# Second layer's input projection: 512-column groups, per-row-block weight tiles, three token tiles side by side

## The chip, the cores and the metric

The kernel runs on one core of one Trainium2 chip. The metric is the device time of one execution in microseconds (us), taken as the median of several runs. Engines go by the profile's short names: PE (TensorE matmul) and PEld (its weight loads), DVE (VectorE), ACT (ScalarE), POOL (GpSimd) and SP (SyncE, which here only issues DMAs).

## What is computed

One inference step of a two-layer encoder on a prompt of 2048 tokens and a sample of 32 tokens, width 1024. Only the second layer's projections, its gates and the 32-token attention are rewritten by the change:

```python
def fox_layer(x, k_prefix, v_prefix, logf_prefix, norm_g, w_in, b_forget, qn_g, kn_g, w_out):
    n, t, _ = x.shape
    h = rms_norm(x, norm_g)
    proj = h @ w_in
    q, k, v, gate, fpre = jnp.split(proj, [MIX_C, 2 * MIX_C, 3 * MIX_C, 4 * MIX_C], axis=-1)
    q = rms_norm(q.reshape(n, t, FOX_HEADS, HEAD_DIM), qn_g)
    k = rms_norm(k.reshape(n, t, FOX_HEADS, HEAD_DIM), kn_g)
    v = v.reshape(n, t, FOX_HEADS, HEAD_DIM)
    logf = jax.nn.log_sigmoid(fpre.astype(F32) + b_forget.astype(F32))
    ...
    return x + (attn * jax.nn.silu(gate)) @ w_out, k, v, logf
```

The matrix `w_in` has 4 x 1024 + 16 columns: queries, keys, values, gates and one forget gate for each of 16 heads. The attention that follows weighs keys by a running sum of the forget gates.

## The kernel before

Every float32 product is made of three matmuls: both operands are split into an upper part `hi` and a rest `lo` (`split`, L153: a cast, then a subtraction), and hi x hi, hi x lo and lo x hi are summed in PSUM (the accumulator memory). The width of 1024 is cut into `KT` = 8 row blocks of 128, so that one 128-token tile of one column group takes 24 matmuls.

The second layer's projection is an object of class `Proj` (L174). `load` (L219) reads the transposed, normalized activations `h1T` in 17 transfers (sixteen of 128 tokens and one of 32) through three staging buffers `hst`, and splits each into the resident tiles `h0` to `h5` (ACT casts, DVE subtracts); the 2080 tokens lie in six `PIECES` (256, four times 384, 288). `weights` (L231) reads one column group, row block by row block, through three staging buffers `wst`, multiplies each by the norm's weight (L242), and splits it into one large tile `whl` that holds the whole group. There are two such tiles: while one is multiplied, the next is filled, by POOL alone save for the first group (DVE and ACT).

There are sixteen groups of 256 columns: four of values (V; the last has 16 forget-gate columns more), four of queries (Q), four of keys (K), four of gates (G). For V, Q and K, `token_major` (L259) takes two token tiles at a time, into the two halves of one PSUM bank of 512 columns (`pm`, four banks), 48 matmuls of 256 columns; the sample's 16 matmuls come last. V's results are copied out (L774, ACT), split and stored. Q's and K's go through `head_norm` (L306: square on ACT L309, reduce L311, small steps, a product L314 on DVE, a product L315 on POOL) and one step later through `turn` (L321), four transposes per bank, a split into `qhl` and stores to `qT` or `kT`. Between V and Q stands the log-forget section: its small tiles have a pool of their own, its two matmul pairs and three transposes (L829, L830, L841) share PSUM with others.

For the gates, `col_chunk` (L289) makes the transposed product: 128 gate columns by one piece of tokens, 24 matmuls, 48 units in all. Between units runs `sample_pair` (L900), the 32-token attention for a pair of heads, as a generator in six steps, eight pairs, one begun every four units. Each engine carries out its instructions in the order of its list, which a scheduler made; SP's list holds nearly all DMAs.

The three buffers of a pair that matter below, as they are before:

```python
            pr = wk.tile([2 * NS, 5 * P], F32, name="prs", tag="prs")
            ...
            ph = wk.tile([P, 5, 2 * NS], F32R, name="phs", tag="phs")
            ...
            op = wk.tile([2 * NS, P], F32, name="ops", tag="ops")
```

## Time and profile before

| what | value |
|---|---|
| runs | 2676.01, 2676.89, 2681.09 us (median 2676.89) |
| profiled execution, first to last instruction (span) | 2675.6 us |
| PE busy in the span | 2586.7 us, 97% |
| PEld, DVE, ACT, POOL busy | 88%, 60%, 44%, 43% |
| second layer's V, Q, K projections | about 821 to 1424 us in the span |
| its gates | about 1424 to 1639 us |
| last: attention and output projection | 1639 to 2676 us |

The profiled execution's span is 1.3 us below the median of the three runs; what lies around the span is not more than that. Busy shares are averages over stages with different limits, so a stage is read by its own stretch of the trace.

### The profile page before, as it was taken

The page shows a single profiled execution, that of the slowest core. Times are in us where ns is not written, and L with a number is a line of the kernel's source. Part 1 is how long each engine was busy: PE and PEld are TensorE (multiplying, and loading weights), DVE is VectorE, ACT ScalarE, POOL GpSimd, SP SyncE. Part 2 cuts the span into 40 slices and gives each one's busy share as a digit, 9 for nine tenths or more (in the row PEclk, how much of TensorE's full clock was granted, in tenths as well). Part 3 has the DMA queues.
Part 4 walks back from the last instruction along what each step waited for, and adds up shares of the span by engine and source line. Part 5 has one row for each costly group of instructions (what it writes and reads, how often), then busy time and mean ns, then how long its engine had stood idle before and what let it go on. Part 6 is the DMA issues. An engine that isn't in the chain of part 4 may idle for free. (4 is left out here: it accounts for less than half of the span.)

```text
span 2675.6 us, 47345 instructions
## 1 busy us (share of the span) xinstructions
PE 2586.7 (97%) x17259; PEld 2345.5 (88%) x17259; DVE 1604.6 (60%) x3847; ACT 1166.4 (44%) x2424; POOL 1149.9 (43%) x1583
## 2 busy tenths in 40 slices
PE   6999999799998999999999999999999999999999
PEld 6999999688887999999999998887888878877787
DVE  7650244778765115554553324889988988888521
ACT  5321111556554122222222114777777777777310
POOL 4454240455534434554554422555555555553100
PEclk9999999799998999999999999999999999999999
DMA  6342110976738443445555316544354455443642
GB/s 187 101 110 88 44 47 23 211 185 169 181 100 266 161 159 97 105 111 132 144 146 139 94 62 162 145 113 122 97 148 120 102 120 141 111 103 90 194 149 75
DMA packets 314120, 338.14 MB, mean 126 GB/s; under 512 B 32311, under 2 KB 263887, under 8 KB 313886
## 3 DMA queue, kind: packets, MB, share of 16 engines
q1 hardware_dynamic: 233550, 242.82, 31.6%
q0 software_dynamic: 76320, 87.98, 15.1%
q10 hardware_dynamic: 4016, 4.31, 0.5%
q8 instruction: 136, 2.23, 0.4%
q14 instruction: 98, 0.80, 0.1%
HBM read 203.05 MB, written 132.06 MB: 125 GB/s over the span
## 5 line engine op out<-in xcount | busy, mean ns | idle before, releaser
L271 PE MATMUL pm<-whl,h 128*128 128x256 f32 (+1 forms) x5760 | 713.7, 283 | 6.3 <-ACT h L155 3.1
L271 PEld LDWEIGHTS pm<-whl,h 128*128 128x128 f32 x5760 | 694.9, 190 | 7.9 <-ACT h L155 3.5
L296 PE MATMUL pm<-h,whl 128*128 128x384 f32 (+2 forms) x2880 | 472.3, 322 | 0.0
L296 PEld LDWEIGHTS pm<-h,whl 128*128 128x128 f32 x2880 | 455.3, 188 | 1.8
L158 POOL TENSOR_TENSOR pl<-pf,ph 128x512 fp32r<-128x512 f32 (+3 forms) x270 | 303.6, 1127 | 263.5 <-DVE ph L157 253.2
L1058 ACT ACTIVATE pr<-pr,mnf 128x128 f32<-128x128 f32 (+15 forms) x256 | 309.6, 1211 | 61.6 <-DVE mnf L1053 60.6
L1077 PE MATMUL pt<-ident,pr 128*128 128x128 f32 x2176 | 323.3, 274 | 5.5 <-DVE pl L158 5.4
L1077 PEld LDWEIGHTS pt<-ident,pr 128*128 128x128 f32 x2176 | 251.2, 141 | 39.3 <-DVE pl L158 11.4
L158 DVE TENSOR_TENSOR pl<-pt,ph 128x512 fp32r<-128x512 f32 (+3 forms) x436 | 261.4, 612 | 39.8 <-ACT ph L155 36.7
L1048 PE MATMUL ps<-ka,qs 128*128 128x512 f32 (+3 forms) x640 | 253.6, 397 | 16.9 <-DVE mnf L1053 15.9
L1053 DVE CUSTOM_DVE_ANT_0 pr<-ps,cb 128x1024 f32<-128x1024 f32 (+7 forms) x256 | 248.8, 981 | 17.9 <-PE ps L1049 9.2
L155 ACT CAST ph<-pt 128x512 fp32r<-128x512 f32 (+3 forms) x436 | 224.9, 529 | 60.9 <-PE pt L1077 44.0
L1070 PE MATMUL pa<-pl,vhl 128*128 128x512 f32 (+3 forms) x640 | 249.2, 395 | 2.3 <-POOL pl L158 2.3
L1070 PE MATMUL pa<-ph,vhl 128*128 128x512 f32 (+3 forms) x640 | 243.6, 383 | 3.8 <-DVE ph L157 3.2
L1049 PE MATMUL ps<-kb,qs 128*128 128x512 f32 (+3 forms) x640 | 228.8, 366 | 0.0
L1082 ACT COPY pf<-pt 128x512 f32<-128x512 f32 (+3 forms) x270 | 140.3, 523 | 66.9 <-PE pt L1077 63.9
L157 DVE CAST ph<-pf 128x512 fp32r<-128x512 f32 (+3 forms) x270 | 143.9, 537 | 35.8 <-ACT pf L1082 35.7
L577 PE MATMUL po<-wo,mh 128*128 128x512 f32 x512 | 162.9, 398 | 0.8 <-ACT mh L155 0.5
L1048 PEld LDWEIGHTS ps<-ka,qs 128*128 128x128 f32 x640 | 121.2, 189 | 46.5 <-DVE mnf L1053 30.3
L157 POOL CAST whl<-wst 128x256 fp32r<-128x256 f32 (+1 forms) x184 | 73.3, 420 | 186.3 <-PE pm L281 105.5
L242 POOL TENSOR_SCALAR wst<-wst,g1c 128x256 f32<-128x256 f32 (+1 forms) x120 | 115.5, 968 | 88.2 <-DMA wst<-in_w_in_dram 86.4
L311 DVE TENSOR_REDUCE ssh<-sq 128x8 f32<-128x512 f32 (+3 forms) x99 | 62.4, 630 | 137.3 <-ACT sq L309 137.2
(396 smaller groups left out, 4050.9 us busy)
## 6 DMA issues: line engine op xcount, KB each, us to landing
qT<-qhl SPq DMA_DIRECT2D x192, 128.0 KB, 2.4
qs<-qT POOLq DMA_DIRECT2D x48, 512.0 KB, 7.3
wst<-in_w_in_dram SPq DMA_DIRECT2D x168, 128.0 KB, 2.6
kT<-qhl SPq DMA_DIRECT2D x128, 128.0 KB, 2.4
ka<-kT POOLq DMA_DIRECT2D x32, 512.0 KB, 7.1
kb<-kT POOLq DMA_DIRECT2D x64, 256.0 KB, 9.0
cb<-cT SPq DMA_DIRECT2D x32, 512.0 KB, 9.6
vhl<-vH POOLq DMA_DIRECT2D x32, 512.0 KB, 4.7
```

Source lines behind the costliest of these rows:

```text
L155: nc.scalar.copy(hi, src)
L157: eng_hi.tensor_copy(hi, src)
L158: eng_lo.tensor_tensor(out=lo, in0=src, in1=f32(hi), op=ALU.subtract)
L271: nc.tensor.matmul(ps[:, j, :], a[:, kt, :], b[:, kt, :], start=(i == 0), stop=(i == 3 * KT - 1))
L296: nc.tensor.matmul(ps, a[:, kt, c:c + P], b[:, kt, :], start=(i == 0), stop=(i == 3 * KT - 1))
L577: nc.tensor.matmul(ps, a[:, kt, :], wo[kt][:, b, cs], start=(i == 0), stop=(i == 3 * KT - 1))
L1048: nc.tensor.matmul(ps[:, s0:s0 + m], lhs, ka[:, ks], start=True, stop=False)
L1049: nc.tensor.matmul(ps[:, s0:s0 + m], lhs, kb[:, ks], start=False, stop=not diag)
L1053: nc.vector.tensor_tensor_reduce(out=pr[:, c0:c0 + n], in0=ps[:, :n], in1=cb[:, :n], scale=1.0, scalar=mns[-1][:, 0:1] if mns else 3e38, o ...
L1058: nc.scalar.activation(pr[:, :L], pr[:, :L], AF.Exp, bias=mns[-1][:, 0:1], scale=-1.0, accum_out=sm)
L1070: nc.tensor.matmul(pa[:, r0 * P:], vhl[b], pp[:, r0:].rearrange("p r q -> p (r q)"), start=(b == 0 and i == 0), stop=(b == nkb - 1 and i = ...
L1077: nc.tensor.transpose(pt[:, r, :], prs[r][:, b * P:(b + 1) * P], ident)
```

## The change

The second layer uses a new class `WideProj`; the first layer, the attention and the output projections stay as they are.

- Groups: V in 384, 384 and 256 + 16 columns; Q, K and G in two groups of 512 each: nine groups in place of sixteen.
- Weights: ten tiles `whl`, each for one row block of one group (8 in use, 2 spare). The first two row blocks of the next group are made early, in the spare tiles; block k + 2 is written when the matmuls of the group's last token tile (or last gate unit) have used block k. Even blocks are made by POOL, odd ones by DVE, ACT and DVE; the very first group goes through DVE and ACT. Staging has two buffers `wst`, not three.
- Order of matmuls: the first three token tiles (or gate units) of a group are accumulated at the same time in three banks, row block by row block; the others one after the other. The sample comes before the last token tile.
- Each bank now holds one token tile of up to 512 columns, and `turn_wide` turns one token tile: four transposes, and stores with runs of 128 tokens (512 bytes) instead of 256 tokens.
- `load` writes straight into the `lo` tile and splits in place, with no staging buffers. It stands behind the first group's weights, as before.
- Memory: the log-forget section takes its tiles out of the two `qhl` buffers; in `sample_pair`, `prs`, `phs`, `pls` and `ops` share buffers with `ckp`, `khi`, `klo` and `qps`; the gates' `sg` has two buffers, not three.

```diff
         def load(self, srcT):
...
+            for c0, n in [(c0, P) for c0 in range(0, NTOK, P)] + [(NTOK, NS)]:
+                hi = self.at(0, c0, n)
+                lo = self.at(1, c0, n)
+                nc.sync.dma_start(f32(lo), srcT[:, c0:c0 + n].rearrange("(k p) t -> p k t", p=P))
+                split(hi, lo, f32(lo), nc.scalar, nc.vector)
...
+    class WideProj(Proj):
+        SPARE = 2
+        LEAD = 3
+
+        def slot(self, k, fast):
+            cols = self.plan[0]
+            width = sum(n for _, n in cols)
+            hl = self.wp.tile([P, 2, self.cw], F32R, name="whl", tag="whl", bufs=KT + self.SPARE)[:, :, :width]
+            st = self.wp.tile([P, self.cw], F32, name="wst", tag="wst", bufs=2)[:, :width]
...
+                nc.sync.dma_start(st[:, at:at + n], self.w[k * P:(k + 1) * P, c0:c0 + n])
...
+            (nc.vector if fast else nc.gpsimd).tensor_scalar_mul(st, st, self.g[:, k:k + 1])
+            split(hl[:, 0], hl[:, 1], st, *((nc.scalar, nc.vector) if fast else (nc.gpsimd, nc.gpsimd)))
...
+        def prefetch(self, plan, fast=False):
...
+            for k in range(KT):
+                self.slot(k, True)
+
+        def next_weights(self):
+            self.w8, self.ahead = self.ahead, []
+            for k in range(self.SPARE if self.plan else 0):
+                self.slot(k, False)
...
+        def freed(self, k):
+            if self.plan and k + self.SPARE < KT:
+                self.slot(k + self.SPARE, k % 2 == 1)
...
+            lead = [psum() for _ in range(self.LEAD)]
+            for kt in range(KT):
+                for t in range(self.LEAD):
+                    self.token_mms(lead[t], t, kt)
+            for t in range(self.LEAD):
+                out(lead[t], t)
...
+            ps = psum()
+            for kt in range(KT):
+                self.token_mms(ps, NT - 1, kt)
+                self.freed(kt)
...
-        pj = Proj(es, w_in1, g1c, "c", CW + 16, "right")
+        pj = WideProj(es, w_in1, g1c, "c", 512, "right")
...
+        vcols = [[(2048, 384)], [(2432, 384)], [(2816, 256), (4096, 16)]]
+        pj.prefetch(vcols + [[(b + c * 512, 512)] for b in (0, 1024, 3072) for c in range(2)])
         pj.load(h1T)
...
+                self.t = [pj.ev.tile([P, 1024], F32, name="lf", tag="qhl", bufs=2) for _ in range(2)]
...
-            pr = wk.tile([2 * NS, 5 * P], F32, name="prs", tag="prs")
+            pr = wk.tile([2 * NS, 5 * P], F32, name="prs", tag="ckp")
...
-            ph = wk.tile([P, 5, 2 * NS], F32R, name="phs", tag="phs")
-            pl = wk.tile([P, 5, 2 * NS], F32R, name="pls", tag="pls")
+            ph = wk.tile([P, 5, 2 * NS], F32R, name="phs", tag="khi")
+            pl = wk.tile([P, 5, 2 * NS], F32R, name="pls", tag="klo")
...
-            op = wk.tile([2 * NS, P], F32, name="ops", tag="ops")
+            op = wk.tile([2 * NS, P], F32, name="ops", tag="qps")
```

Three places where the instruction lists show the change. The first is SP's list where the second layer begins, before the change. `hst` is a load of 128 tokens of activations, `wst` one of a weight block, `h1T` the store of the last activations.

```order
L239 DMA wst_9401<-in_w_in1_dram 128x256
L239 DMA wst_9406<-in_w_in1_dram 128x256
L239 DMA wst_9411<-in_w_in1_dram 128x256
L223 DMA hst_9444<-h1T_66 128x8x128
L728 DMA h1T_66<-hT_9279 128x8x128
L223 DMA hst_9448<-h1T_66 128x8x128
L223 DMA hst_9452<-h1T_66 128x8x128
L239 DMA wst_9416<-in_w_in1_dram 128x256
```

And the same place of SP's list after the change, where the activations go straight to `h0`, `h1` and so on.

```order
L348 DMA wst_9401<-in_w_in1_dram 128x384
L348 DMA wst_9407<-in_w_in1_dram 128x384
L838 DMA h1T_66<-hT_9279 128x8x128
L348 DMA wst_9413<-in_w_in1_dram 128x384
L348 DMA wst_9419<-in_w_in1_dram 128x384
L348 DMA wst_9425<-in_w_in1_dram 128x384
L348 DMA wst_9431<-in_w_in1_dram 128x384
L348 DMA wst_9437<-in_w_in1_dram 128x384
L348 DMA wst_9443<-in_w_in1_dram 128x384
L225 DMA h0_9373<-h1T_66 128x8x128 x2
L225 DMA h1_9374<-h1T_66 128x8x128 x3
```

The first three activation loads stood behind three weight blocks; now all of them stand behind all eight, which pass through two staging buffers.

The second place is PE's list in the first Q group, before: `pm` is a bank of two token tiles, `pss` and the `pt` of L841 belong to the log-forget section.

```order
L271 MATMUL pm_11920<-whl_11056,h1_9374 128x256 x24
L271 MATMUL pm_11920<-whl_11056,h2_9375 128x256 x17
L841 MATMUL pt_11709<-ident_87,off_11691 128x128
L829 MATMUL pss_11725<-lsh_11721,upper_11651 128x80
L830 MATMUL pss_11725<-lsh_11721,ones_11654 128x80
L271 MATMUL pm_11920<-whl_11056,h2_9375 128x256 x7
L271 MATMUL pm_11997<-whl_11056,h2_9375 128x256 x12
L841 MATMUL pt_11714<-ident_87,off_11691 128x128
```

And after: banks 11359 to 11361 are token tiles 0 to 2, side by side, 11502 is tile 3 and 11555 is tile 4.

```order
L376 MATMUL pm_11359<-whl_11247,h0_9373 128x512 x3
L376 MATMUL pm_11360<-whl_11247,h0_9373 128x512 x3
L376 MATMUL pm_11361<-whl_11247,h1_9374 128x512 x3
L376 MATMUL pm_11502<-whl_11238,h1_9374 128x512 x2
L376 MATMUL pm_11502<-whl_11247,h1_9374 128x512 x3
L971 MATMUL pt_11322<-ident_87,lf_11273 128x128
L959 MATMUL pss_11334<-lf_11273,lf_11272 128x80
L960 MATMUL pss_11334<-lf_11273,lf_11272 128x80
L971 MATMUL pt_11326<-ident_87,lf_11273 128x128
L376 MATMUL pm_11555<-whl_10673,h1_9374 128x512 x3
```

The log-forget transposes stood among a bank's 48 matmuls; now they stand together, with tile 3 already used up ahead of them, and tile 4 (which takes the bank of tile 0) behind them.

The third place is PE's list at a sample pair's beginning among the gates, before: `ckp` and `qps` are the pair's keys and queries as loaded, `ops` is the pair before's result.

```order
L296 MATMUL pm_18915<-h2_9375,whl_17965 128x384 x8
L917 MATMUL pss_18948<-ident_87,ckp_18902 128x128 x4
L918 MATMUL pss_18948<-ident_87,ckp_18902 128x32
L919 MATMUL pss_18948<-ident_87,qps_18905 128x32
L296 MATMUL pm_18969<-h3_9376,whl_17965 128x384 x8
L964 MATMUL pt_18944<-ident_87,ops_18900 128x64
```

And after, at the switch to the second gate group: banks 16363 to 16365 are its three units side by side, 16525 the fourth, `whl_16326` is row block 6 and `whl_16335` row block 7.

```order
L1047 MATMUL pss_16010<-ident_87,ckp_15964 128x128 x4
L1048 MATMUL pss_16010<-ident_87,ckp_15964 128x32
L426 MATMUL pm_16363<-h0_9373,whl_16326 128x256 x2
L426 MATMUL pm_16364<-h0_9373,whl_16326 128x256 x2
L426 MATMUL pm_16365<-h0_9373,whl_16326 128x256 x2
L426 MATMUL pm_16525<-h0_9373,whl_16326 128x256 x2
L1094 MATMUL pt_16006<-ident_87,ops_15962 128x64
L1049 MATMUL pss_16010<-ident_87,qps_15967 128x32
L426 MATMUL pm_16363<-h0_9373,whl_16326 128x256
```

The transpose of the loaded `qps` stood ahead of the transpose of the old `ops`; now it stands directly behind it, and the two tiles share one buffer.

## Rows read from the trace of the kernel before

**Rows 1.** The page's first part: busy time, share of the span, instructions.

```profile
PE 2586.7 (97%) x17259; PEld 2345.5 (88%) x17259; DVE 1604.6 (60%) x3847; ACT 1166.4 (44%) x2424; POOL 1149.9 (43%) x1583
```

**Rows 2.** Windows: busy time of each engine, then granted clock, DMA share, GB/s.

```profile
850.00:1050.00 200.00, 200.00 (x1662) 199.90 (x1662) 54.38 (x149) 47.26 (x101) 76.74 (x108) 1.00 0.48 155
1050.00:1425.00 375.00, 375.00 (x3182) 375.00 (x3181) 199.70 (x529) 90.18 (x201) 190.93 (x236) 1.00 0.54 128
```

**Rows 3.** Timeline of ACT, copies of V banks: start, duration, what, idle before.

```profile
876.02 0.59 ACT L774 COPY vt<-pm 128x512 f32<-128x512 f32 x1 [5.34 <-PE pm L271]
...
915.96 0.59 ACT L774 COPY vt<-pm 128x512 f32<-128x512 f32 x1 [4.62 <-PE pm L271]
923.55 0.59 ACT L774 COPY vt<-pm 128x512 f32<-128x512 f32 x1 [5.34 <-PE pm L271]
```

**Rows 4.** Timeline of ACT, head norms' squares of Q and K banks.

```profile
1250.78 0.60 ACT L309 ACTIVATE sq<-pm 128x512 f32<-128x512 f32 x1 [1.84 <-PE pm L271]
...
1269.18 0.60 ACT L309 ACTIVATE sq<-pm 128x512 f32<-128x512 f32 x1 [3.52 <-PE pm L271]
```

**Rows 5.** Timeline of ACT, gate units of 384 columns.

```profile
1603.94 0.49 ACT L982 ACTIVATE sg<-pm 128x384 f32<-128x384 f32 x1 [3.82 <-PE pm L296]
...
1633.25 0.49 ACT L982 ACTIVATE sg<-pm 128x384 f32<-128x384 f32 x1 [3.69 <-PE pm L296]
```

**Rows 6.** Timeline of DVE, second output projection, 24 matmuls of 512 columns each.

```profile
2557.52 0.69 DVE L1205 TENSOR_TENSOR op<-ps,op 128x512 f32<-128x512 f32 x1 [3.13 <-PE ps L1196]
...
2595.60 0.69 DVE L1205 TENSOR_TENSOR op<-ps,op 128x512 f32<-128x512 f32 x1 [4.75 <-PE ps L1196]
```

**Rows 7.** Timeline of SP's issues where the second layer begins.

```profile
796.52 2.21 SPq L239 DMA_DIRECT2D wst<-in_w_in_dram  x3
802.16 0.38 SPq L223 DMA_DIRECT2D hst<-h1T  x1
...
808.61 9.13 SPq L239 DMA_DIRECT2D wst<-in_w_in_dram  x6
```

**Rows 8.** Timeline of PE in the same stretch.

```profile
817.46 0.80 PE L271 MATMUL pm<-whl,h 128*128 128x256 f32 x2 [3.09 <-ACT h L155]
820.93 11.33 PE L271 MATMUL pm<-whl,h 128*128 128x256 f32 x78 [2.67 <-DVE h L158]
```

**Rows 9.** Timeline of DVE in the same stretch.

```profile
807.97 0.41 DVE L158 TENSOR_TENSOR whl<-wst,whl 128x256 fp32r<-128x256 f32 x1
...
811.53 0.75 DVE L720 TENSOR_SCALAR hn<-xr,br 128x1024 f32<-128x1024 f32 x1 [2.00 <-POOL br L150]
...
825.84 1.23 DVE L158 TENSOR_TENSOR h<-hst,h 128x1024 fp32r<-128x1024 f32 x1 [1.08 <-ACT h L155]
```

**Rows 10.** Windows of that stretch, columns as in Rows 2.

```profile
822.00:824.00 2.00, 2.00 (x11) 2.00 (x11) 2.00 (x4) 0.00 (x0) 1.85 (x3) 0.50 0.89 244
824.00:826.00 2.00, 2.00 (x15) 2.00 (x14) 0.92 (x2) 1.05 (x1) 0.48 (x1) 0.73 1.08 303
```

**Rows 11.** Groups of POOL by form, 1050 to 1425: busy, mean ns, idle before.

```profile
L242 POOL TENSOR_SCALAR wst<-wst,g1c 128x256 f32<-128x256 f32 x56 | 51.2, 924 | 14.3 <-DMA wst<-in_w_in_dram 14.0
L158 POOL TENSOR_TENSOR whl<-wst,whl 128x256 fp32r<-128x256 f32 x56 | 40.2, 740 | 0.0
...
L157 POOL CAST whl<-wst 128x256 fp32r<-128x256 f32 x58 | 21.6, 402 | 24.1 <-PE pm L281 24.1
```

**Rows 12.** Groups of POOL by form, 1640 to 2600.

```profile
L158 POOL TENSOR_TENSOR pl<-pf,ph 128x512 fp32r<-128x512 f32 x195 | 252.3, 1294 | 186.5 <-DVE ph L157 176.4 <-PE pt L1077 9.5
```

**Rows 13.** DMA issues, 800 to 1640: count, size, median us from issue to landing.

```profile
wst<-in_w_in_dram SPq DMA_DIRECT2D x125, 128.0 KB, 2.7
...
hst<-h1T SPq DMA_DIRECT2D x16, 512.0 KB, 5.6
...
ckp<-in_cache_fox_k_dram SPq DMA_DIRECT2D x8, 256.0 KB, 3.1
...
qps<-q SPq DMA_DIRECT2D x8, 16.0 KB, 2.3
```

**Rows 14.** Groups of DVE by form, 1050 to 1425.

```profile
L314 DVE TENSOR_TENSOR hno<-pm,rr 128x512 f32<-128x512 f32 x59 | 40.7, 689 | 8.4 <-DVE rr L134 3.7 <-PE pt L326 0.4 <-DMA wst<-in_w_in_dram 0.4
L311 DVE TENSOR_REDUCE ssh<-sq 128x8 f32<-128x512 f32 x59 | 40.5, 686 | 103.7 <-ACT sq L309 103.6
L133 DVE SCALAR_TENSOR_TENSOR rt<-rt,rv 128x8 f32<-128x8 f32 x59 | 13.2, 225 | 2.0
```

More of the change, by code (lines that the diff above doesn't have):

```diff
@@ L332, in turn, with turn_wide @@
+    def turn_wide(pt, ev, o, t, h0, dstT):
+        pt = pt.rearrange("p (h t) -> p h t", h=4)
+        for hp in range(4):
+            nc.tensor.transpose(pt[:, hp], o[:, hp * P:(hp + 1) * P], ident)
+        hl = ev.tile([P, 2, 4, P], F32R, name="qhl", tag="qhl", bufs=2)
+        split(hl[:, 0], hl[:, 1], pt, nc.scalar, nc.vector)
+        for hh in range(2):
+            for w in range(2):
+                store(dstT[h0 + hh:h0 + 8:2, w, :, t * P:(t + 1) * P].rearrange("h d t -> d h t"),
                       f32(hl[hh * HD:(hh + 1) * HD, w]))
@@ L971, in hybrid_step_kernel @@
         unit = 0
-        for gc in range(4):
+        for gc in range(2):
             if gc:
-                whi, wlo = pj.next_weights()
+                pj.next_weights()
+                first = pj.col_chunks([(cc * P, 0) for cc in range(pj.LEAD)])
             for tch in range(NTC):
-                for cc in range(2):
-                    r0 = gc * CW + cc * P
-                    ps = first if unit == 0 else pj.col_chunk(whi, wlo, cc * P, tch)
+                for cc in range(4):
+                    r0 = gc * 512 + cc * P
+                    ps = first.pop(0) if first else pj.col_chunks([(cc * P, tch)], tch == NTC - 1 and cc == 3)[0]
                     c0, n = PIECES[tch]
-                    sg = pe.tile([P, TCH], F32, name="sg", tag="sg", bufs=3)[:, :n]
+                    sg = pe.tile([P, TCH], F32, name="sg", tag="sg", bufs=2)[:, :n]
                     nc.scalar.activation(sg, ps, AF.Tanh, scale=0.5)
```

149 lines of the change are left out of this document (104 added, 45 removed).

## The prediction

> **What bounds the kernel now.** I read the page's busy shares first: PE 97%, everything else far below [rows 1]. An average can hide a stage with another limit, so next come the windows of the stage that is changed: PE is busy for all of 850 to 1050 and all of 1050 to 1425, at full clock, with DVE at 27% and 53% and POOL at 38% and 51% [rows 2]. So in V, Q and K nothing but PE's own list sets the end. Faster matmuls there are worth their full difference, and every wait that PE does not have today is a loss of its full length. The working therefore has two halves: what PE's list gets shorter by, and where PE will have to wait.
>
> **The saving.** The pace of the old matmuls is read where PE sets the beat of another engine. Seven gaps between V copies last 39.94 us, 5.706 us for the 48 matmuls of a bank of 256 columns, 118.9 ns each; the gap with the sample's 16 matmuls in it is 7.59, so these take 1.88 [rows 3]. In Q and K three gaps last 18.40, 6.133 each, which is 48 matmuls and four transposes of together 0.43 [rows 4]. For 384 columns there are the gate units: seven gaps in 29.31, 4.187 for 24 matmuls, 174.5 ns [rows 5]. For 512 columns the nearest is the second output projection, whose operands alternate in the same hi, hi, lo pattern: seven gaps in 38.08, 5.44 for 24, 226.7 ns [rows 6]. Two matmuls of 256 thus cost 237.8 and one of 512 226.7: 11 ns are saved for each that goes.
> - V: three groups of 256 took 3 x 8 x 5.706 = 136.9; two of 384 take 2 x 16 x 4.187 = 134.0. The group of 272 is as it was. Saved 2.9.
> - Q and K: 8 groups x 8 x 5.706 = 365.2; 4 groups x 16 x 5.44 = 348.2. Saved 17.0. The transposes are 256 before and after.
> - Sample: 12 x 1.88 = 22.6; by the same paces 16 x (2 x 0.1745 + 0.125 + 4 x 0.2267) = 22.1. Saved 0.5.
> - Gates: the same 1152 matmuls of the same pieces. Nothing.
>
> Sum: 20.4 us, 0.76%. Bounds of the 512 pace: if each fell only as the step from 256 to 384 says (55.6 ns for 128 columns, so 230.1 for 512) the saving would be 15.2; more than 20.4 no row gives.
>
> A rule stands against this. "TensorE: Matmul & The Clock Gate", section Back-to-back issue gap, of the Trainium skill puts the gap of an isolated matmul at columns / 2.4 + 2.5 ns. By it only 2.5 ns would go with each of 1920 matmuls fewer, 4.8 us in all. The trace does not agree at 256 columns: it has 118.9 ns where the rule has 109.2.
>
> **Where PE will wait.** (1) The start. Before, three weight blocks were issued at 796.5, an activation load from 802.16, and the remaining blocks took SP until 817.7 [rows 7]; PE ran without a gap from 820.93 [rows 8]. After, SP's list puts all eight blocks ahead of the first activation load, through two buffers: blocks 2 and 3 wait for the subtractions of 0 and 1 (before, these ended at 808.4 [rows 9]), land about 2.7 later [rows 13], and are scaled behind DVE's 811.53 instruction; with cast and subtraction blocks 4 and 5 are issued at about 813.4, blocks 6 and 7 one such round later at 818.1, the first activations at 818.7. These land 4 to 5 us later (5.6 is the median with three in flight [rows 13]), are cast and then subtracted (1.23 [rows 9], and not much less for the cast): PE runs from about 825.5, 4.6 late. Between 3 (it lands early) and 8 (it waits its turn behind 0.4 MB of weights). Behind that wait on SP stand the other loads and V's first stores: 0.5, from 0 to 3.
>
> (2) Weights at a switch. T is the end of the old group's last matmul. PE needs block k of the new group 9k matmuls later, 2.04 us per block at 512 columns. POOL makes blocks 2, 4, 6: scaling and cast of 512 are taken as twice those of 256, 1.85 and 0.80 [rows 11], the subtraction is 1.29 [rows 12], 3.9 together; the load of 256 KB takes 3.1, as `ckp` of that size [rows 13]. Block 2 is loaded and scaled ahead; its place is free at T - 4.8 (the last tile's 24 matmuls take 5.44), so it is ready at T - 2.7 and gives up its staging buffer. Block 4 follows 7.0 later at T + 4.3 (needed at 8.2), block 6 at T + 11.3 (needed at 12.2). It just holds: 0.5 each for Q's second group and K's two. In V the same sum with 384 and 272 columns leaves block 6 late by 0.35 and 0.55: 0.9. For the first gate group a unit's share is 9 x 0.119 = 1.07 per block, so block 6 would be wanted at 6.4; five late turns (2.1) and the fourth unit's first 18 matmuls (2.1) stand in between, so 10.6 against 11.3: 0.7. DVE's odd blocks are quicker and fit. Bounds: 0 (the next tile's matmuls fill in), and 8 in all.
>
> (3) The first Q group, where the scheduler has used tile 3 up as filler. Tile 4 needs tile 0's bank, which is free when the square (0.60 [rows 4]), the reduction (0.69), some ten small steps of about 0.2 and the product (0.69) [rows 14] are done, on a DVE list that also holds a second and third reduction and the log-forget sums: about 6. PE has 11 matmuls of 512 and some transposes left to cover that, 3. Taken 3.0, between 0 and 8. Before, these log-forget steps lay between 48 matmuls of a bank and cost PE nothing.
>
> (4) The second gate group. Its last unit of 288 columns lasts 3.2, so block 2 is ready at T - 0.7, block 6 at T + 13.3 and wanted at 6.4; unit 3 (2.1) and a sample pair's work (about 2) are in between: 2.8 of waiting. Here `qps` is loaded into the buffer of `ops`, whose transpose stands in the row ahead: the whole 2.3 us of that load [rows 13] shows, but at the time at which PE lacks block 6 anyway. Taken 2.8, between 1 and 6.
>
> (5) The end of the gates. Sharing buffers sets the sample pairs one behind another; the last pair's `ops` transpose is the row before the attention. POOL's loads for the attention stand behind that pair's `vlo`, as far as I can count 10 to 14 us before the end, about as early as now. Taken 0, up to 5.
>
> (6) Costs that lie under other work. The stores of Q and K have shorter runs, but the DMA share in that stage is 0.54 [rows 2]. DVE and ACT take over half the weights; DVE is at 53% there and ACT below that [rows 2]. The two `sg` buffers hold back units only if DVE is late by a whole unit.
>
> Waits: 4.6 + 0.5 + 1.5 + 0.9 + 0.7 + 3.0 + 2.8 = 14.0. Net 20.4 - 14.0 = 6.4 less than the profiled 2675.6: 2669.2. The median of the runs is 1.3 above that span, so I expect **2670.5**, 0.24% faster. A measurement here can tell about 0.2%, 5.4 us, from no change.
>
> **The clock.** After PE had idled and then begun at 820.93, the window 822 to 824 had a granted clock of 0.50 and the next one 0.73 [rows 10]: some 3.8 us at the lower level (1.2 GHz), 1.9 lost. Today that is paid at the start anyway. A stall of about 3 us at (3) and (4) may cost it once more each. I put nothing in the sum, and 4 in the range.
>
> **The rivals.**
> - *All waits but the start are hidden* (fillers fit, the loads are quicker than `ckp`): 20.4 - 5 = 15 less, 2661. For it: the margins in (2) are positive for Q and K. Against it: (3) and (4) are short of matmuls by count. Chance 0.14.
> - *The stalls eat the saving* (the upper halves of 1, 3, 4 and two half-clock spells): 2674 to 2682. For it: idle PE did show 0.50. Chance 0.13.
> - *Slower: the weight chain is late at every switch.* Blocks 4 and 6 each need a load that SP issues behind stores which wait for DVE or ACT. Each 1 us per round makes 2 us per switch, 16 over eight switches. From 0.8 us per round the kernel is slower than before by over 0.2%; at 1.2 it is 2670.5 + 19 = 2689. For it: the margin at block 6 is 0.9 us, and SP's list has turned heads' stores between the blocks. Against it: an issue takes SP some 0.4 us [rows 7], and these stores belong to tiles long done. Chance 0.22.
> - *A matmul of 512 costs here what two of 256 cost* (three banks side by side, other operands than in the output projection): Q and K save nothing, 2670.5 + 17.0 = 2687.5. Against it: 226.7 ns is the mean of 168 matmuls [rows 6]. Chance 0.05. By the Trainium skill's gap rule, "TensorE: Matmul & The Clock Gate", Back-to-back issue gap, it would be 2670.5 + 15.6 = 2686, much the same.
>
> **How the numbers follow.** My forecast has 0.46, with a range of its own from 2664 to 2676; two thirds of it lie below 2671.5. Faster: 0.30 + 0.14 = 0.44. Same: 0.16 + 0.13 + 0.01 = 0.30. Slower: 0.22 + 0.04 = 0.26. Leaving out the last part of the best case and the upper half of the slower ones, the range is 2658 to 2690.
>
> **What would show it.** Tile 3 to 14 of a Q or K group should come every 5.44 + 0.43 = 5.87 us, V tiles every 4.19. PE should start without gaps at about 825.5 with SP's first activation load near 818.7. PE's idle should lie in the first Q group behind the log-forget transposes and at the second gate group's row block 6, about 3 us each. If tiles come slower than 5.9, the saving is wrong; if PE idles over 2 us at each switch on POOL's blocks 4 and 6, the slower rival holds.

## The result and the profile after

The changed kernel takes 2721.59 us (median of four runs, 2720.39 to 2727.49), the kernel before 2678.99 in the same session (four runs, 2676.01 to 2686.05): a ratio of 1.0161, 95% interval 1.0142 to 1.0179. It is 43 us slower where 6 faster was forecast, and outside the range. The profiled execution has a span of 2718.7, against 2675.6.

The page's first line answers to [rows 1]: PE has 2000 instructions fewer, and is busy for 4 us more.

```profile
PE 2590.8 (95%) x15259; PEld 2258.8 (83%) x15259; DVE 1638.7 (60%) x3870; ACT 1177.9 (43%) x2449; POOL 1036.1 (38%) x1339
```

Next the windows from the first matmul of Q to the first of the gates, and from there to the first of the attention; columns as in [rows 2]. First the kernel before:

```profile
1015.20:1424.10 408.90, 408.90 (x3465) 408.80 (x3464) 224.22 (x608) 98.57 (x218) 212.12 (x262) 1.00 0.52 124
1424.10:1639.50 215.40, 215.40 (x1431) 205.89 (x1430) 63.16 (x187) 42.30 (x87) 81.15 (x158) 1.00 0.42 117
```

and the changed one:

```profile
1022.70:1446.00 423.30, 407.92 (x1850) 323.38 (x1848) 235.96 (x605) 100.96 (x217) 153.92 (x125) 0.99 0.42 113
1446.00:1683.00 237.00, 222.35 (x1448) 209.28 (x1445) 77.13 (x201) 44.56 (x94) 64.40 (x112) 0.99 0.46 125
```

PE had no idle time in either stretch. Now it has 423.30 - 407.92 = 15.4 us in Q and K and 237.00 - 222.35 = 14.7 in the gates, 30 together. Q and K grew by 14.4, the gates by 21.6; Q's first matmul comes 7.5 later, and what follows the gates takes as long as before (1035.7 against 1036.1). So three places make the 43 us. Less expected: the time in which PE is busy hardly fell in Q and K (407.9 against 408.9), though 1536 matmuls of 512 replaced 3072 of 256.

The squares of head norm show the pace of tiles, as in [rows 4] (timeline of ACT):

```profile
1181.58 0.60 ACT L309 ACTIVATE sq<-pm 128x512 f32<-128x512 f32 x1 [3.20 <-PE pm L376]
...
1187.61 0.60 ACT L309 ACTIVATE sq<-pm 128x512 f32<-128x512 f32 x1 [2.74 <-PE pm L376]
...
1193.65 0.60 ACT L309 ACTIVATE sq<-pm 128x512 f32<-128x512 f32 x1 [2.27 <-PE pm L376]
```

A tile takes 6.03 us where two halves of a bank took 6.133 [rows 4] and 5.87 were forecast. Less 0.43 for the transposes, 24 matmuls take 5.60, 233 ns each, not 226.7 [rows 6].

What PE waits for from 1020 to 1700 (waits: microseconds in total, how often, longest):

```profile
PE pm L376 <- DVE hno L314: 10.6, 7, 3.2
PE pss L1049 <- DMA qps<-q: 4.4, 2, 2.8
PE pm L426 <- DVE hno L314: 2.5, 2, 1.7
PE pm L376 <- DVE lf L964: 2.2, 1, 2.2
PE pt L436 <- DVE qhl L160: 2.0, 2, 1.6
PE ps L1179 <- DVE sg L1114: 1.8, 1, 1.8
PE pss L1047 <- DMA ckp<-in_cache_fox_k_dram: 1.6, 1, 1.6
PE pm L426 <- DVE sg L1114: 1.6, 1, 1.6
PE pt L971 <- DVE lf L962: 0.9, 1, 0.9
PE pm L376 <- POOL whl L160: 0.9, 2, 0.6
```

Weights (`whl`) stand last in this list. The largest is `hno`, the buffer of normalized heads, of which there are three. One such wait, behind the first three tiles of K's first group, whose fourth needs the bank of Q's last tile; from the timelines of DVE, SP, POOL and PE:

```profile
1246.98 1.70 DVE L160 TENSOR_TENSOR whl<-wst,whl 128x512 fp32r<-128x512 f32 x1 [0.69 <-ACT whl L157]
1248.61 0.67 DVE L314 TENSOR_TENSOR hno<-so,rr 32x512 f32<-32x512 f32 x1
1248.71 0.81 SPq L348 DMA_DIRECT2D wst<-in_w_in_dram  x2
1251.64 1.57 POOL L350 TENSOR_SCALAR wst<-wst,g1c 128x512 f32<-128x512 f32 x1 [3.50 <-DMA wst<-in_w_in_dram]
1253.17 1.26 POOL L315 TENSOR_TENSOR hno<-hno,gqf 32x512 f32<-32x512 f32 x1
1254.46 0.34 SPq L1006 DMA_DIRECT2D q<-hno  x1
1256.18 0.69 DVE L314 TENSOR_TENSOR hno<-pm,rr 128x512 f32<-128x512 f32 x1 [2.60 <-DMA q<-hno]
1256.93 3.30 PE L376 MATMUL pm<-whl,h 128*128 128x512 f32 x13 [2.86 <-DVE hno L314]
```

Read upwards: PE waits for a bank; the bank's product L314 waits for a free `hno`; that buffer holds the sample's heads and is free when their store has landed; the store stands behind the sample's product on POOL; and POOL, which takes its list in order, had stood 3.5 us with a weight block in front of that product, waiting for the block's bytes. DVE had the sample's `hno` done at 1249.3. By the count of blocks the weight block is one of the two that are made early for the group after this one. Its load was issued only at 1248.71, when DVE's subtraction (1246.98 + 1.70) gave back one of the two staging buffers; before the change there were three. PE waits for no weight here, and yet the weights' place in POOL's list delays a bank.

The start, to be held against [rows 7, 8] (timelines of SP, ACT, PE):

```profile
818.90 14.38 SPq L225 DMA_DIRECT2D h<-h1T  x9
824.52 1.04 ACT L157 CAST h<-h 128x1024 fp32r<-128x1024 f32 x1 [2.01 <-DMA h<-h1T]
826.88 5.49 PE L376 MATMUL pm<-whl,h 128*128 128x384 f32 x16 [0.25 <-DVE h L160]
```

And windows around an idle time of 3.19 us of PE that ended at 1150.11, columns as in [rows 2]:

```profile
1148.00:1150.00 2.00, 0.00 (x0) 0.00 (x0) 0.63 (x2) 0.00 (x0) 2.00 (x3) 0.94 0.38 97
1150.00:1152.00 2.00, 1.89 (x5) 1.51 (x6) 2.00 (x6) 0.81 (x2) 2.00 (x3) 0.50 0.27 71
1152.00:1154.00 2.00, 2.00 (x8) 1.62 (x7) 2.00 (x4) 0.21 (x1) 2.00 (x2) 0.71 0.49 123
1154.00:1156.00 2.00, 2.00 (x10) 1.62 (x9) 1.97 (x12) 0.21 (x1) 0.64 (x2) 1.00 0.51 139
```

After the idle time the granted clock is 0.50 (the lower level, 1.2 GHz) for 3.4 us and the matmuls start 426 ns apart, so 1.7 us are lost beside the 3.19. The trace has three such spells in Q, K and gates, 5.1 us lost.

### The profile page after: what moved, and what is told of

It is laid out like the page before. It is cut to its first block, busy times and chain, and to the rows that moved or that the text cites. A ratio compares the mean times of both kernels' runs of the same rounds, so it can differ in the third digit from the quotient of the medians.

```text
span 2718.7 us, 43054 instructions
## 1 busy us (share of the span) xinstructions
PE 2590.8 (95%) x15259; PEld 2258.8 (83%) x15259; DVE 1638.7 (60%) x3870; ACT 1177.9 (43%) x2449; POOL 1036.1 (38%) x1339
## 5 line engine op out<-in xcount | busy, mean ns | idle before, releaser
L376 PE MATMUL pm<-whl,h 128*128 128x512 f32 (+2 forms) x2688 | 564.8, 369 | 27.3 <-DVE hno L314 10.6
L376 PEld LDWEIGHTS pm<-whl,h 128*128 128x128 f32 x2688 | 470.5, 190 | 98.2 <-DVE hno L314 14.4
L1179 PE MATMUL ps<-ka,qs 128*128 128x512 f32 (+3 forms) x640 | 253.6, 397 | 16.9 <-DVE mnf L1184 14.3
L1184 DVE CUSTOM_DVE_ANT_0 pr<-ps,cb 128x1024 f32<-128x1024 f32 (+7 forms) x256 | 249.0, 981 | 17.9 <-PE ps L1180 11.9
L1201 PE MATMUL pa<-pl,vhl 128*128 128x512 f32 (+3 forms) x640 | 249.6, 396 | 2.4 <-POOL pl L160 2.3
L271 PE MATMUL pm<-whl,h 128*128 128x256 f32 x1152 | 143.6, 283 | 0.6 <-DVE h L216 0.4
## 6 DMA issues: line engine op xcount, KB each, us to landing
cb<-cT SPq DMA_DIRECT2D x32, 512.0 KB, 10.6
```

The lines of the kernel that those rows point to most:

```text
L376: nc.tensor.matmul(ps, a[:, kt, :], self.w8[kt][:, b], start=(kt == 0 and i == 0), stop=(kt == KT - 1 and i == 2))
L1179: nc.tensor.matmul(ps[:, s0:s0 + m], lhs, ka[:, ks], start=True, stop=False)
L1184: nc.vector.tensor_tensor_reduce(out=pr[:, c0:c0 + n], in0=ps[:, :n], in1=cb[:, :n], scale=1.0, scalar=mns[-1][:, 0:1] if mns else 3e38, o ...
L1201: nc.tensor.matmul(pa[:, r0 * P:], vhl[b], pp[:, r0:].rearrange("p r q -> p (r q)"), start=(b == 0 and i == 0), stop=(b == nkb - 1 and i = ...
```

## The experiments

The theory after these rows (T): 30 us of PE's idle time come from shared things at a switch of groups (buffers, and lists that are taken in order), not from weights that come too late. The rivals: the weight chain is late (the forecast's slower rival); the three tiles side by side give DVE three banks at once; a matmul of 512 simply costs what two of 256 cost.

All are edits of the changed kernel. Times are of one execution each, but for before, changed, e8, e9 and e17, which have four (median). Lengths and idle times are read from PE's rows of each trace: Q and K from their first matmul to the gates' first, the gates from there to the attention's first, and within each PE's idle time ahead of its rows. e10 and e11, which turned out to change nothing, show how far single executions differ: Q and K by 2 us, the gates by 6.5.

| kernel | time us | Q and K | PE idle | gates | PE idle |
|---|---|---|---|---|---|
| before | 2678.99 | 408.9 | 0.0 | 215.3 | 0.0 |
| changed | 2721.59 | 423.2 | 15.4 | 237.0 | 14.7 |
| e1_hno4 | 2727.17 | 415.2 | 9.1 | 249.6 | 17.8 |
| e2_bank5 | 2723.07 | 424.1 | 12.3 | 235.7 | 13.4 |
| e3_ops | 2710.48 | 422.1 | 14.2 | 229.7 | 8.6 |
| e4_halves | 2744.26 | 443.8 | 22.1 | 235.6 | 12.7 |
| e5_prod | 2719.40 | 418.6 | 12.5 | 238.8 | 14.9 |
| e6_swap | 2716.75 | 422.9 | 14.6 | 236.1 | 11.6 |
| e7_lead1 | 2726.93 | 419.4 | 13.1 | 243.7 | 15.1 |
| e8_best1 | 2724.90 | 420.6 | 12.8 | 243.2 | 17.7 |
| e9_best2 | 2718.50 | 416.0 | 11.2 | 242.2 | 18.4 |
| e10_pad | 2727.85 | 422.5 | 14.3 | 242.0 | 16.2 |
| e11_order | 2729.47 | 421.6 | 14.0 | 243.5 | 16.8 |
| e12_nowt | 2712.57 | 415.6 | 9.6 | 231.5 | 10.6 |
| e13_nowt_lead1 | 2704.99 | 412.9 | 8.3 | 231.0 | 10.3 |
| e14_nosample | 2710.16 | 414.8 | 9.4 | 235.1 | 12.5 |
| e15_lead1_buffers | 2714.57 | 415.7 | 11.9 | 241.9 | 16.2 |
| e16_startq | 2718.92 | 421.1 | 13.1 | 239.0 | 16.9 |
| e17_final | 2720.98 | 417.1 | 11.5 | 239.6 | 15.5 |
| e18_nowt_nosample | 2715.93 | 417.9 | 8.9 | 231.5 | 10.7 |

**One buffer or bank more.** A fourth `hno`:

```diff
+        pj.hb = 4
...
-                vt = pj.ev.tile([P, 384], F32, name="vt", tag="hno", bufs=3)[:, :cw]
+                vt = pj.ev.tile([P, 384], F32, name="vt", tag="hno", bufs=4)[:, :cw]
```

> Four buffers for the head norm's product (hno), not three; nothing else. Theory M (results leave too late): at each group switch of Q and K the next tile's bank is held because the product L314 finds no free hno buffer, since the sample's product waits on POOL behind a weight block and its store. Then PE's waits on DVE hno in Q and K (about 13 us by the profile of the changed kernel) shrink to under 5, the Q and K stage falls from 423.2 us to about 414, the span from 2718.7 to about 2709. Rival B (banks): four banks with one tile each are too few whatever the buffers; then the stage stays above 420 and the waits on hno move by under 3 us.

A fifth bank for the tiles side by side:

```diff
-            lead = [psum() for _ in range(self.LEAD)]
+            lead = [self.pa.tile([P, 512], F32, name="pm", tag="pas")[:, :width]] + [psum() for _ in range(self.LEAD - 1)]
...
+        pj.pa = p_a
```

> A fifth PSUM bank: the first tile of each lead goes into the bank that the sample attention uses later; hno keeps three buffers. Theory M: a fifth bank covers one tile (5.9 us) of lateness, so the waits before tile 3 or 4 (2 to 3 us each in Q and K) vanish, those before the last tile stay: stage about 415. Rival W (weights are late): the waits move to the weight blocks of POOL and the stage stays at 420 to 423.

The attention's `ops` in a buffer of its own, not that of `qps` (a small pool is closed earlier for its room):

```diff
-            op = wk.tile([2 * NS, P], F32, name="ops", tag="qps")
+            op = wk.tile([2 * NS, P], F32, name="ops", tag="ops")
```

> The result ops of a sample pair has a buffer of its own, so that the next pair's qps load no longer waits for the transpose of ops (room comes from closing the forget-gate tiles' pool with the projections). Theory S (shared buffers): PE's waits on the load of qps, 1.62 and 2.80 us, vanish, with about 1 us of half clock behind the second: gates 237.0 to about 231.5. Rival: PE lacks weight block 6 at the same time and the bank's or pair's next step anyway; then the gates stay within 2 us of 237.

The fourth buffer takes 8 us from Q and K; the bank does nothing for their length. In e2 the waits of about 3 us at the switches are gone but for one of 2.4, yet PE now waits some 0.15 us for `hno` ahead of many a tile in the middle of a group, and those tiles come 6.45 us apart, not 6.03. It is `hno` that holds the tiles. But the gates of e1 are 12.6 longer: its trace has 3.1 more of idle time there and five half-clock spells, 27 us in all (PE busy for some 22 of them) where the changed kernel has one of 3.4, which is worth some 9.5. Nothing is left of the 8. `ops` takes 7 from the gates, little more than the 6.5 by which single executions differ there, but the idle time (8.6) is well below that of e10 and e11 (16.2 and 16.8); before this edit `qps` could be loaded only when the row ahead of it on PE had read `ops`. In e3 that wait is gone from PE's list over the gates, and the turns of K's last tiles lead it:

```profile
PE pt L436 <- DVE qhl L160: 3.1, 2, 1.6
PE pm L426 <- DVE hno L314: 2.5, 2, 1.6
```

**The width of the matmuls.** Each 512-column tile of Q and K is multiplied in two halves of 256, in the same bank:

```diff
-        def token_mms(self, ps, t, kt):
+        def token_mms(self, ps, t, kt, half=0):
+            cut = ps.shape[-1] // 2 if ps.shape[-1] == 512 else ps.shape[-1]
+            cs = slice(half * cut, (half + 1) * cut)
```

> The changed kernel with every 512-column matmul of the projections cut into two of 256, one half of the bank after the other; weights, buffers and tiles as in the change. Only the pace of the tiles in the middle of a Q or K group is to be read. If 512 columns save 11 ns over two of 256, as the prediction had it from the output projection, such a tile comes every 6.03 + 24 x 0.011 = 6.30 us. If they save 2 to 3 ns, as the starts of the matmuls in the profile suggest (234 against 118 ns), every 6.09 to 6.12 us.

Tiles come every 6.12 us, as two halves of a bank did before the change:

```profile
1098.52 0.60 ACT L309 ACTIVATE sq<-pm 128x512 f32<-128x512 f32 x1 [2.15 <-PE pm L378]
1104.64 0.60 ACT L309 ACTIVATE sq<-pm 128x512 f32<-128x512 f32 x1 [3.50 <-PE pm L378]
```

So 512 columns save 0.09 to 0.10 us of a tile's 24 matmuls, 4 ns for each one that goes: with 64 tiles 6 to 7 us in Q and K. e4's own length says nothing of the pace: in its order a group's first halves want all eight blocks in half the time, and its blocks come free only in the second halves, so PE waits 20.6 us for POOL's `whl` from 1020 to 1710 (15.7 in Q and K, 4.9 in the gates). So blocks that are wanted in half the time are late. Two edits ask where the 7 ns per matmul between this stage and the output projection come from.

```diff
-            hl = self.wp.tile([P, 2, self.cw], F32R, name="whl", ...
+            hl = self.wp.tile([P, 2, self.cw + 4], F32R, name="whl", ...
```

> The two halves of a weight tile lie 2064 bytes apart and not 2048, nothing else changes. If 233 ns for a 512-column matmul come from where its operands lie in memory, the steady interval of tiles falls from 6.03 us towards 5.87 (the output projection's 227 ns). If it belongs to the matmuls of this stage whatever their address, 6.03 stays and the whole run is within 5 us of the changed kernel's 2722.

```diff
-            for i, (a, b) in enumerate(((hi, 0), (hi, 1), (lo, 0))):
+            for i, (a, b) in enumerate(((hi, 0), (lo, 0), (hi, 1))):
```

> The three matmuls of a row block go hi, lo, hi of the activations in place of hi, hi, lo, so that no two neighbours share a stationary operand. If a repeated stationary operand matters to the pace, the steady interval of tiles moves from 6.03 us by a tenth or more. If the pace depends on the 512 columns alone, it stays at 6.03.

Squares come 6.01 and 6.05 us apart: neither address nor order. What makes the difference stays open.

**The sample's chain and the tiles side by side.** Products with the head scales on DVE:

```diff
-                    o = pj.head_norm(ps[:, 0]..., P, 8, gB, nc.gpsimd)
+                    o = pj.head_norm(ps[:, 0]..., P, 8, gB, nc.vector)
```

> The head norm's product L315 goes to DVE; POOL keeps only weight blocks in Q and K. Three hno buffers as in the change. Theory M says that the sample's product stands on POOL behind a block that waits for its load, so that its store, the free hno buffer and the last tile's bank come late: without POOL's queue in that chain the two waits of about 3 us before tile 3 (second Q group, first K group) go, and the Q and K stage falls from 423.2 to about 415, the gates by 2 to 3 us from 237.0. Rival D: DVE has 64 x 0.69 = 44 us more to do in 423 and holds the banks itself; the stage stays or grows.

The sample's evacuation behind the last tile's:

```diff
-            evac_s(so)
             out(ps, NT - 1)
+            evac_s(so)
```

> In each group the last token tile's results are taken out ahead of the sample's, not behind them; nothing else. Theory M: the last tile no longer waits for the sample's product and store, so the waits before tile 3 shrink, as far as the last tile's product does not now wait for a turn: stage 423.2 to about 416. Rival: the three hno buffers are all taken by tiles that wait for their turns; then the wait moves to another tile and the stage stays within 3 us.

One token tile ahead, by the program:

```diff
-        LEAD = 3
+        LEAD = 1
```

> One token tile (or gate unit) at a time from the start of each group, no three side by side. Rival W (the new group's weight blocks are late, and only three tiles side by side hide it): a tile asks for a block every 0.7 us, while POOL makes blocks 4 and 6 about 7 us apart, so PE waits 7 to 10 us on POOL's whl at each of eight switches: the span grows by 50 us or more. Theory M alone (results leave too late because three tiles end together): the waits on hno go and the span falls. I expect both: waits on hno nearly gone, waits on whl of some 50 us in their place.

Q and K move by 4.6, 0.3 and 3.8 us, the whole kernel by no more than single executions differ. But e7 is no test of tiles one by one. The scheduler puts the matmuls of two more tiles between those of the first while the blocks are still being made, so that after the switch to Q's second group three squares stand close together again, as in the changed kernel (1145.11, 1146.52, 1150.92). Only e13 below, where no block is made, has them a tile apart. First e7, then e13 (timelines of ACT):

```profile
1143.70 0.60 ACT L309 ACTIVATE sq<-pm 128x512 f32<-128x512 f32 x1 [2.17 <-PE pm L376]
1145.11 0.60 ACT L309 ACTIVATE sq<-pm 128x512 f32<-128x512 f32 x1 [0.81 <-DVE ssh L311]
1146.95 0.60 ACT L309 ACTIVATE sq<-pm 128x512 f32<-128x512 f32 x1
```

```profile
1128.31 0.60 ACT L309 ACTIVATE sq<-pm 128x512 f32<-128x512 f32 x1 [3.26 <-PE pm L377]
1134.36 0.60 ACT L309 ACTIVATE sq<-pm 128x512 f32<-128x512 f32 x1 [3.65 <-PE pm L377]
```

So the 1.1 us for which PE waits on POOL's `whl` in e7 do not show that blocks would be in time for tiles one by one. Against the slower rival stand the 0.9 us of such waits in the changed kernel, not e7.

**Together.** e8 has the fourth `hno`, `ops` in the buffer of `cbs`, a third `sg` and the swap; e9 also the products on DVE:

> Four changes to the changed kernel at once: a fourth buffer for normalized heads, the attention's ops tile in the buffer of cbs and no longer in that of qps, a third sg buffer, and the sample's product behind the last tile's. If the loss is idle TensorE behind shared buffers, the gains of the single runs (8 us of Q and K with the fourth buffer, 10 of the span with ops apart, some 3 with the swap) add up, with 2 for sg: about 2700 us, Q and K 412 to 416 us long, gates 222 to 228. Rival: each wait that goes lets the next one through, or PE falls to half clock somewhere else: above 2711 us, with idle PE in Q, K and gates of more than 20 us still (30 in the changed kernel).

> As e8_best1, and the product with the head scales on DVE in place of POOL. POOL then is free for the weight blocks, DVE has more of the list that frees banks. If POOL's queue (sample product behind a weight block) is what still holds the banks, 4 us less than e8_best1, as Q and K lost 4.6 with it alone; if DVE's list is the next limit, the same as e8_best1 or a few us more.

Ratios to before: 1.0167 (1.0151 to 1.0182) and 1.0151 (1.0131 to 1.0172), much as the changed kernel's; the two intervals overlap. What helped alone did not add up; the first form of T, that buffers are the cause, falls. PE's waits in e8 show the same time under other names:

```profile
PE pt L436 <- DVE qhl L160: 6.9, 4, 2.7
PE pss L1065 <- DVE klo L160: 6.5, 2, 5.5
```

The longest, in the second gate group (timelines of DVE and PE):

```profile
1587.92 0.64 DVE L350 TENSOR_SCALAR wst<-wst,g1c 128x512 f32<-128x512 f32 x1 [3.06 <-DMA wst<-in_w_in_dram]
...
1589.25 1.95 DVE L160 TENSOR_TENSOR whl<-wst,whl 128x512 fp32r<-128x512 f32 x1 [0.28 <-ACT whl L157]
...
1592.59 0.72 DVE L160 TENSOR_TENSOR klo<-pss,khi 128x544 fp32r<-128x544 f32 x1 [0.76 <-ACT khi L157]
...
1593.37 0.69 PE L1065 MATMUL pss<-khi,qhi 128*64 128x512 f32 x1 [5.52 <-DVE klo L160]
```

It is POOL's case over again on DVE: a weight block waits 3.06 us for its bytes at the head of the list, then takes 1.95 for its subtraction, and the small steps that come before `klo` (the rest of the pair's keys), which PE needs, stand behind it.

**What the chain consists of.** From Q's second group on, no weight work at all:

```diff
-            self.w8, self.ahead = self.ahead, []
-            for k in range(self.SPARE if self.plan else 0):
+            if self.ahead:
+                self.w8, self.ahead = self.ahead, []
+            for k in range(self.SPARE if len(self.plan) > 5 else 0):
...
-            if self.plan and k + self.SPARE < KT:
+            if len(self.plan) > 5 and k + self.SPARE < KT:
```

> From Q's second group on no weight is loaded or prepared: all five later groups use the tiles of Q's first, so their outputs are other numbers, and the matmuls are as many as before. If TensorE idles because the block by block preparation sits on POOL, DVE and ACT at the same moment as a group's last evacuations, the idle of Q, K and gates falls from 30 us to under 12 and the span by 20 us or more, to 2700 or less. If the evacuations alone are too slow at a switch (three tiles finish together, sample and last tile behind them), idle stays over 24 us and the span above 2712.

> As e12_nowt, and only one token tile ahead at the start of a group, so that tiles finish one by one. If the bunch of three tiles holds PE, idle in Q and K falls by 4 us or more against e12_nowt; if the weight work was all, the two are within 3 us.

No norm for the sample's rows of Q and K:

```diff
-                    o = pj.head_norm(so.rearrange("p (h d) -> p h d", d=HD), NS, 8, gB, nc.gpsimd)
-                    oo = o.rearrange("p h d -> p (h d)")
+                    oo = so
```

> The sample's 32 rows of Q and K are stored as they are, without the norm over heads, so their numbers are others. Its square, reduction, Newton steps, two products and one buffer of normalized heads per group fall away. If the sample's chain at a group's end is what holds the last tile and tiles 1 to 3 of the next group, Q and K lose 7 us or more of their 423 (the fourth buffer took 8). If not, under 3 us.

Both at once:

> The edits of e12_nowt and e14_nosample together: five groups on Q1's weights and no norm for the sample's rows of Q and K, so outputs are other numbers. If weight work and the sample's chain are two separate causes of PE's idle time in Q and K (15.4 us, of which each took about 6), about 3.5 us of it are left, which is the log-forget wait of the first Q group (3.1), and Q and K last 407 to 410. If both are the same queue, idle stays at 8 or more.

Without weight work Q and K are 7.6 us shorter and idle 5.8 less; without the sample's chain 8.4 and 6.0; without both 5.3 and 6.5. By e18's expectation 8 or more left mean one queue, and 8.9 are left; but 2.6 of them are a new kind of wait. In each group's later tiles PE waits 0.15 us a tile for `hno`, and such tiles come 6.45 us apart, not 6.03 (timeline of PE in e18):

```profile
1195.33 5.16 PE L377 MATMUL pm<-whl,h 128*128 128x512 f32 x21 [0.15 <-DVE hno L314]
...
1201.79 5.16 PE L377 MATMUL pm<-whl,h 128*128 128x512 f32 x21 [0.16 <-DVE hno L314]
```

At the switches 6.3 us are left, against 8.9 in e12 and 8.7 in e14. So weight work and the sample's chain overlap in part, as in the rows where a weight block stands ahead of the sample's product; by how much is not shown. Over Q, K and gates e12's idle time is 20.2, between the two cases of its expectation: weight work is a third of the 30. What is left in e12 is short in Q and K and long at the end of the gates (PE's waits, 1010 to 1710):

```profile
PE pm L377 <- DVE hno L314: 6.1, 8, 0.9
PE pss L1050 <- DMA qps<-q: 5.5, 1, 5.5
PE pss L1065 <- DVE klo L160: 2.6, 1, 2.6
PE pm L377 <- DVE lf L965: 2.0, 1, 2.0
```

The longest `hno` wait falls from 3.2 to 0.9; two of some 0.85 us are left at each switch, one ahead of the last tile and one behind the next three. The log-forget wait stays. In e13, where tiles end one by one, the same waits of 0.85 us stand at the same places, and idle in Q and K differs from e12's by 1.3 us: three tiles side by side cost nothing by themselves there. In the gates an idle time of 10.6 is left without any weight work, all of it at the last pair, whose steps now have no gate unit to run beside. The first and longest of these waits is on `qps`, which shares a buffer with `ops`; no kernel without weight work had `ops` apart, so the sharing's part of it is not shown. Around these waits the granted clock is 0.50 for 17.1 us, of which PE is busy for 10.6, so that some 5 are lost (window of e12, columns as in [rows 2]):

```profile
1660.00:1677.00 17.00, 10.55 (x47) 7.68 (x48) 6.06 (x24) 4.23 (x11) 3.65 (x6) 0.50 1.41 315
```

Even e13, with no weight work and tiles one by one, has Q and K at 412.9, and is slower than before by 27.7 us (2704.99 against 2677.34 beside it); 15.7 of these are in the gates, where it has the same idle time at the last pair and the same long spell behind it (20.5 us).

**The start, and a last combination.** The first three activation loads on POOL's queue:

```diff
-                nc.sync.dma_start(f32(lo), srcT[:, c0:c0 + n]...
+                (nc.gpsimd if c0 < 3 * P else nc.sync).dma_start(f32(lo), srcT[:, c0:c0 + n]...
```

> The first three activation loads are issued by POOL's queue and no longer stand on SP's behind the eight weight blocks. If that place on SP sets the start of V (first load 818.9, PE from 825.6), PE starts 4 us or more earlier, at 821 or before. If the loads wait for memory of layer 0 or for the weight blocks' bytes, the start stays within 2 us of 825.6.

From the timelines of POOL, SP, ACT and PE, and the list of DMA issues from 795 to 835 (median us from issue to landing):

```profile
811.52 2.75 POOL L225 DMA_DIRECT2D h<-h1T  x3 [1.28 <-issue]
819.48 10.92 SPq L225 DMA_DIRECT2D h<-h1T  x7
825.21 1.04 ACT L157 CAST h<-h 128x1024 fp32r<-128x1024 f32 x1 [0.88 <-DMA h<-h1T]
828.94 1.01 PE L377 MATMUL pm<-whl,h 128*128 128x384 f32 x2 [15.53 <-ACT h L157]
```

```profile
h<-h1T POOLq DMA_DIRECT2D x3, 512.0 KB, 6.6
```

The three loads are issued 7.4 us earlier than in the changed kernel (811.52 against 818.90), and their bytes land by about 821, 6.6 us behind their issue; yet PE begins 3.3 us later (828.94 against 825.62). In ACT's list the casts of the fourth and fifth tiles, which SP still loads, now stand ahead of the first tile's: the cast at 825.21 waits for SP's first load, and the first tile's is the third in line. So e16 does not test whether the place on SP sets the start: the bytes came sooner, and the order of the casts undid it.

e15 has the edit of e7, four `hno`, three `sg` and `ops` in the buffer of `cbs`; e17 the edit of e7, four `hno`, `ops` alone and the loads of e16:

> One tile ahead, four buffers of normalized heads, ops in the buffer of cbs, three of sg: every wait for a shared buffer that the traces showed is eased, and nothing finishes in a bunch. Buffers and bunches as the whole cause give 2700 us or less; if weight work beside the evacuations is the cause, 2712 or more, as e8_best1 with 2724.9.

> One tile ahead, four buffers of normalized heads, ops in a buffer of its own, and the first three activation loads on POOL's queue. Each was worth 8 to 10 us somewhere when tried alone, or is thought to be worth 4. If what the runs showed holds together, 2695 to 2705; if the waits move on as in e8_best1, 2712 or more.

e17 has a ratio of 1.0156 (1.0136 to 1.0176). PE waits no more for `qps` in it, as in e3, but its gates last 239.6: the 7 us of e3 are not there. e15, in one execution, is 7 us under the changed kernel. No version found comes near the kernel before. Making the two early blocks in the middle of a group was not tried; e12 and e13, with no blocks at all, show that it would not be enough. Nor was a third staging buffer, the one that the change took away, though the load in the rows of K's first group waited for one.

## Why the prediction was wrong, by its own steps

**The saving of Q and K: mis-sized.** 17.0 us were forecast; the pace gives 64 x (6.133 - 6.03) = 6.6. The number came from the output projection [rows 6], the lower bound from the step between 256 and 384 columns was 230 ns, and the truth was above both, 233. Here the Trainium skill ("TensorE: Matmul & The Clock Gate", Back-to-back issue gap) was nearer in its difference: 2.5 ns for each matmul that goes, against 4 measured and 11 taken. The estimate by its figures for an isolated matmul, 512 / 2.4 + 2.5 = 215.8 ns, does not agree with the 233 of this trace. The rival built on it (2686) is short too, since the pace is some 10 us of a miss of 51.

**(1) The start, V's 2.9 and the sample's 0.5.** PE ran without a gap from 826.88, 6.0 later than before [rows 8], where 4.6 was forecast; the first activation load at 818.90 (818.7 forecast) fits step (1). That the place on SP is the cause is not shown, as e16 also changed the order of casts. From there to Q's first matmul V takes 195.8 us against 194.3, where 2.0 less was forecast (2.9 saved, 0.9 waited): its tiles of 384 columns do come 4.16 us apart (4.19 forecast), but PE waits 2.7 us on their evacuation (`vh`), which was in no step. In all Q's first matmul comes 7.5 later, where 3.1 was forecast. The sample's 0.5 can't be read apart.

**(2) Weight blocks at a switch.** Right as to PE: it was to wait 2.2 us for weights in Q, K and gates, and waits 0.9 for POOL's. So the slower rival was right in its sign and wrong in its mechanism, though e4, where blocks are wanted sooner, waits 20.6 us for them.

**(3) The first Q group.** 3.0 forecast, 2.2 + 0.9 = 3.1 measured, on DVE's list with its log-forget steps. Right.

**(4) The second gate group.** 2.8 forecast; 3.9 measured (three waits from 1573.8 on), but on the pair's loads and `klo`, not on row block 6.

**(5) The end of the gates.** 0, up to 5; measured 2.8 on `qps` and 1.8 on `sg`, 4.6. For the 2.8 the shared buffer that the step named is the cause (gone in e3).

**(6) "Costs that lie under other work": the step that failed.** It looked at the load of DVE and ACT as shares, 53%, found room, and put the cost at nothing. Of 30 us of idle time in Q, K and gates some 17 are waits for `hno`, `qhl` and a mid-stage `sg`, for which the sum has no term. Of the 13.1 us on `hno`, 7.0 are gone in e12 with the weight work, and 6.1 are left without it, when a switch's evacuations stand alone. Shares hid two things: six of a group's eight weight blocks can only be made from the last tile of the group before it on, and the early two of the group after stand close behind them, so that this work falls just where the last tile, the sample and the next three tiles want the same engines; and a list that is taken in order stands still while its head waits for 256 KB. Before the change POOL prepared a whole group ahead, and such a wait (14.0 us of it in [rows 11]) held nobody up.

**The clock.** 0 in the sum and 4 in the range; three half-clock spells cost 5.1. (At the start [rows 8, 10] give 4.1 us at the lower level from 820.93 on, 2.1 lost, where the forecast read 3.8 and 1.9.)

In Q, K and gates the forecast was -9.5 us and the result +36: idle time 30.0 instead of 8.0 makes 22.0, the pace 10.4, the clock 5.1. Some 8 of these 45 us are spread over first matmuls behind an idle time and over transposes, and are not put down to a cause. Shown by runs are the pace (e4); that weight work at a switch and the sample's norm each hold PE for some 6 us in Q and K, in part the same (e12, e14, e18), and that the holding goes through `hno` (e1); and that `qps` waits for `ops` (e3). What these cost together, and whether a third staging buffer would have freed POOL's list, is not shown. Why eased waits came back elsewhere is shown in one place, `klo` in e8; for the rest of the gates it stays open, as their length also differs by 6.5 us between kernels whose gates are the same.

## What to carry to other kernels

Weight work that is off the critical path is only free while it is done ahead; handed over block by block at the end of a group, it stands in the lists of the engines that evacuate the group, and a block that waits for its bytes holds up the evacuation behind it. An edit of the program's order is not yet one of an engine's list: e7 left the order that it was meant to change, e16 changed another one as well, and only the rows of the engine concerned show it. Before shrinking a double buffer, write out what stands behind each moved instruction on its engine at the switch, and what each shared buffer waits for. A pace taken from another stage is not a bound: take the worst row of that shape, and if the forecast gain hangs on it, keep the case that there is almost none.

## What the runs showed of the hardware

- Matmuls of one shape (128x128 by 128x512, float32) keep 226 to 227 ns in the output projection and 231 to 235 in Q and K, steadily in each place. An offset of 16 bytes between the operand's halves and another order of operands left it so.
- Idle times of PE of 2 to 3 us were followed by 3.4 us at a granted clock of 0.50 at 1050, 1150 and 1660 us, while one of 2.86 us before 1256.93 was not.
- Three activation loads of 512 KB from POOL's queue took 6.6 us (median) from issue to landing in e16, the ten behind them on SP 7.4; at the same place the changed kernel's ten on SP took 7.3.
